# Fourteen warm-up products, delta rule output woven into the attention loop, and alternating 32x32 products in a hybrid decoder block

## The chip, the core and the metric

The kernel runs on one core of a Trainium2 chip. The metric is the device time of one execution in microseconds (us), as the median of several runs. A profile of one execution comes with it. In it PE is TensorE (matmuls), PEld its weight loads, DVE is VectorE, ACT is ScalarE, POOL is GpSimd, and SP is the engine from which nearly all transfers are issued.

## The reference

A decoder block on 512 tokens of width 1024, with 16 learned tokens ahead of them (528 in all): a gated feed-forward layer, a mixer, a second feed-forward layer and a norm. The mixer has two branches on the same normalised input.

```python
h = h + 0.5 * swiglu(rmsnorm(h, ffn1_norm), ...)            # FFN 1, hidden size 2816
u = rmsnorm(h, mix_norm)
c_q, c_kv, k_rope, g_q, g_k, g_v, g_b, g_a, g_z, gate_mla, gate_gdn = split(u @ w_in)
y_mla = mla(c_q, c_kv, k_rope, ...) @ w_mla_o               # 8 heads, causal softmax attention
y_gdn = gated_deltanet(g_q, ..., g_z, ...) @ w_gdn_o        # 8 heads of 64, chunked delta rule
h = h + (sigmoid(gate_mla) * y_mla + sigmoid(gate_gdn) * y_gdn) @ w_out
h = h + 0.5 * swiglu(rmsnorm(h, ffn2_norm), ...)            # FFN 2
# inside gated_deltanet, for each chunk: a triangular system tmat = (I + L)^-1, then
v_new = u_i - w_i @ state
o_i = (q_i * exp(g_i)) @ state + a_i @ v_new
state = state * exp(g_last) + k_dec^T @ v_new
# and at its end
o = rmsnorm(o, gdn_norm) * silu(z)
```

## The kernel before

All tensors lie with channels on the 128 partitions and tokens along the free dimension. A float32 product is made of three products of rounded parts: `weights` casts a slab of weights to its high part `whi` on ACT (L173) and makes the low part `wlo` on DVE (L174), and `mm3` (L201) issues high by high, high by low and low by high. The ring of slabs has three `whi` and three `wlo`, so a new slab's parts wait until the products with the slab three before are through.

The program runs through FFN 1 (to about 370 us), the mixer (to 735), the two branch projections with the gates and the output projection (to 825), FFN 2 (to 1173) and the last norm. Within the mixer the source gives every piece of work a place in a list of slots; a scheduler then writes the order of each engine by the priorities, and a table HOLD adds to it: ('kk', 0, 6, 30) says that the group named kk, number 0, stands behind the matmul with index 30 of input projection 6. Each engine runs its own list in order.

The parts that the change touches:

- The start. Eight products of a block of ones (`warm`, L517) stand ahead of FFN 1's first product `gu`, whose operands `ra` ACT makes from the loaded input (L279). In FFN 1's first tiles four `ssq` products (L268) stand between the `gu` products; they need `sqa`, the sum of the squares of the eight input tiles, made by ACT (`sq`, L235), POOL (L240) and DVE (L248 to L262).
- The output gate z of the delta rule: four projections `z`, each evicted from PSUM by DVE (L651), passed through Silu on ACT, multiplied by the norm's gain `gn` on POOL (L653), and stored to DRAM as `zd`. Their PSUM tile is one of a ring of two ("mm"), their SBUF tile one of a ring of three ("tA").
- `rope_key` rotates the shared key's 32 rows, in halves of 16 partitions: six DVE operations.
- `lower(c)` makes L of chunk c from eight small products `kk` (L872). `solve` inverts its 16x16 blocks by steps of two DVE operations (L895, L897). `merge` builds the inverses of two chunks each from those blocks, with 32x32 products `z1` (L932) and `x12` (L947, L951): all of row group 0 to 31 first, then all of row group 64 to 95. It is called for chunks 1 and 2, and for 3 and 4.
- `scan(c)` is one step of the recurrence: `ks`, then `rr`, eight DVE operations of 64 columns (L976), then `vn`, `oi`, `su`.
- `scan_out()` stands behind the last scan: for each of the four chunks the output `bv` is scaled (L1035), transposed by four products into `yT` (L1040), a PSUM tile of one buffer ("tk"), multiplied with z (`zs`, L1041), and stored as `yd`.
- `attention()` loops over 36 turns of five key blocks each for eight heads: `scores` (products `s`, L1154 to L1159, into the two-buffered PSUM tile "mm"; DVE evicts them to `pr`, L1160), `turn` (transposes `pt`, L1192, L1196), `values` (`o`). Between them it draws single steps of the gate projections (`gate`), whose PSUM tile ("ax") has one buffer and is evicted by DVE to `gt` (L1245).

Of the kernel before, what the change touches and what calls it, by code (L numbers as in the profile page):

```python
# [17 lines left out]
P = 128  # L18
# [22 lines left out]
ROPE = 12.5  # L41
NTAG = {"tA": 3, "tB": 3, "tC": 3, "tD": 4, "kb": 10, "rr": 1, "vn": 2, "vk": 1, "m": 4}
TAG = {n: t for t, ns in {
# [22 lines left out]
CYCLE = (0, 1, 2)  # L66
HOLD = (('nm', 0, 0, 32), ('nm', 1, 0, 36), ('b', 0, 1, 36), ('g', 0, 2, 42), ('tok', 1, 4, 5), ('tok', 2, 5, 4), ('tok', 3, 6, 2), ('tok', 4, 8, 21), ('tok', 7, 10, 0), ('sq', 0, 11, 25), ('vn', 0, 16, 14), ('kvn', 0, 14, 12), ('kvn', 1, 14, 18))
GX = (1,) * 16
# [16 lines left out]
def toff(c):  # L85
    return 0 if c == 0 else NM + P * (c - 1)
# [6 lines left out]
def build(tc, a, out, tap=None):  # L93
# [3 lines left out]
    with ctx:  # L97
# [408 lines left out]
        with tc.tile_pool(name="hid", bufs=1) as hid, tc.tile_pool(name="fp", bufs=2) as fp:  # L506
# [8 lines left out]
            warm = ax_tile("warm")  # L515
            for _ in range(8):
                nc.tensor.matmul(warm[:, 0:P], lhsT=ones, rhs=ones, start=True, stop=True)  # L517
# [130 lines left out]
        def z_tile(i):  # L648
            ps = proj(ZW + i, "z", SEQ)
            z = tmp("z")  # L650
            nc.vector.tensor_tensor(out=z, in0=ps, in1=r[:, NM:NT], op=ALU.mult)  # L651
            table(z, z, AF.Silu)
            nc.gpsimd.tensor_tensor(out=z, in0=z, in1=col("gn").broadcast_to([P, SEQ]), op=ALU.mult)  # L653
            dq.dma_start(zd[i], z)
# [95 lines left out]
        def rope_key():  # L750
            cosk, sink = tmp("cosk", NT, 48), tmp("sink", NT, 48)
            dq.dma_start(cosk, a["cosk"])
            dq.dma_start(sink, a["sink"])
            for x in range(2):
                e1, e2 = tmp("kr1", NT, NM), tmp("kr2", NT, NM)
                m1, m2 = (misc[0:16], misc[32:48])[::1 - 2 * x]
                o1, o2 = ((0, 16), (32, 48))[::1 - 2 * x]
                nc.vector.tensor_tensor(out=e1, in0=m1, in1=cosk[o1[0]:o1[1]], op=ALU.mult)
                nc.vector.tensor_tensor(out=e2, in0=m2, in1=sink[o2[0]:o2[1]], op=ALU.mult)
                nc.vector.tensor_tensor(out=e1, in0=e1, in1=e2, op=ALU.add if x else ALU.subtract)  # L760
                dq.dma_start(krd[16 * x:16 * x + 16], e1)

# [102 lines left out]
        def lower(c):  # L865
# [3 lines left out]
            for h4 in range(4):  # L869
                for hq, ps in enumerate(pk):  # L870
                    h = 2 * h4 + hq
                    nc.tensor.matmul(ps[0:n, h4, 0:n], lhsT=hs(kT, h, o, o + n), rhs=hs(kT, h, o, o + n), start=True, stop=True)  # L872
            for hq, ps in enumerate(pk):
# [36 lines left out]
        def merge(cs):  # L910
# [16 lines left out]
            z1 = sm_tile("z1").rearrange("p (k h s) -> p k h s", k=nk, h=H)  # L927
            for p in range(2):
                s1, s2 = slice(64 * p, 64 * p + 32), slice(64 * p + 32, 64 * p + 64)
                for k, c in enumerate(cs):  # L930
                    for h in range(H):
                        nc.tensor.matmul(z1[s1, k, h], lhsT=L[c][s2, h, s1], rhs=xt[s2, k, h], start=True, stop=True)  # L932
# [9 lines left out]
            x12 = sm_tile("x12").rearrange("p (k h s) -> p k h s", k=nk, h=H)  # L942
            for p in range(2):
                s1, s2 = slice(64 * p, 64 * p + 32), slice(64 * p + 32, 64 * p + 64)
                for k in range(nk):
                    for h in range(H):
                        nc.tensor.matmul(x12[s1, k, h], lhsT=tb[s1, k, h], rhs=nz[s1, k, h], start=True, stop=True)  # L947
                if p == 0:
                    for k in range(nk):
                        for h in range(H):  # L950
                            nc.tensor.matmul(x12[s2, k, h], lhsT=nz[s1, k, h], rhs=tb[s1, k, h], start=True, stop=True)  # L951
                    nc.vector.tensor_copy(t64[32:64, :, :, 0:32], x12[s2])
                for k, c in enumerate(cs):
                    ecopy(EM & 4)(X[c][s1, :, s2], x12[s1, k])
# [13 lines left out]
        def scan(c):  # L968
            n, o = tlen(c), toff(c)
            if c:  # L970
                psk = hd(tk_tile("ks"))
                rr = hd(tok("rr"))
                for i in range(4):
                    nc.tensor.matmul(psk[:, 2 * i:2 * i + 2], lhsT=kT[i][:, o:o + n], rhs=S[:, i], start=True, stop=True)
                for h in range(H):
                    nc.vector.scalar_tensor_tensor(out=rr[:, h], in0=psk[:, h], scalar=nbeg[:, c, h:h + 1],  # L976
                                                   in1=bv[c][:, h * 64:h * 64 + 64], op0=ALU.mult, op1=ALU.add)
                pso = hd(sm_tile("qs"))
# [51 lines left out]
        def scan_out():  # L1030
            nc.vector.scalar_tensor_tensor(out=ro, in0=ro, scalar=1.0 / 64, in1=sq_q[:, 1:5], op0=ALU.mult, op1=ALU.add)
            rsqrt(rn, ro, 1.0, False)
            for c in range(1, 5):
                o, o1 = toff(c), os_[c]
                nc.vector.tensor_tensor(out=o1, in0=o1, in1=hb(rn[:, c - 1], P), op=ALU.mult)  # L1035
                zs = tok("zs").rearrange("p (i t) -> p i t", i=4)
                dq.dma_start(zs, zd[:, :, o - NM:o - NM + P].rearrange("i p t -> p i t"))
                ps = tk_tile("yT").rearrange("p (i t) -> p i t", i=4)
                for i in range(4):
                    nc.tensor.transpose(out=ps[:, i], in_=o1[:, 2 * i:2 * i + 2].rearrange("p h d -> p (h d)"), identity=ident)  # L1040
                nc.vector.tensor_tensor(out=zs, in0=ps, in1=zs, op=ALU.mult)  # L1041
                dq.dma_start(yd[:, :, o - NM:o - NM + P].rearrange("i p t -> p i t"), zs)

# [34 lines left out]
        def keys_values():  # L1078
# [8 lines left out]
            for kc in range(5):  # L1087
# [5 lines left out]
                for i, (c, wk) in enumerate(((ck[0], kvh), (ck[1], kvh), (ck[0], kvl))):  # L1093
                    nc.tensor.matmul(ps, lhsT=c, rhs=wk[:, 4:8].rearrange("p a b -> p (a b)"), start=i == 0, stop=i == 2)
                v = tmp("v", SEQ, n)
# [156 lines left out]
        def attention():  # L1252
# [13 lines left out]
            for t in range(nst + LAG):  # L1266
# [10 lines left out]
                if i < 3:  # L1277
# [270 lines left out]
```

## Time and profile before

| | |
|---|---|
| median of 3 runs | 1191.19 us (1190.66 to 1191.98) |
| profiled execution: its own time | 1191.02 us |
| span of its trace | 1189.2 us |
| busy share of PE, PEld, DVE, ACT, POOL | 98%, 89%, 71%, 46%, 7% |

The span is the time between the first and the last record; the execution's own time has 1.8 us more around it. A record of the trace is one instruction; a float32 product of the small kinds (ones, 32x32) leaves two records. In the rows of a timeline the first number is the start, the second the length of the merged group including the last one's whole duration, and the brackets give the idle time of that engine just before it and who ended it.

### The profile page before, as it was taken

The page shows a single profiled execution, that of the slowest core. Times are in us where ns is not written, and L with a number is a line of the kernel's source. Part 1 is how long each engine was busy: PE and PEld are TensorE (multiplying, and loading weights), DVE is VectorE, ACT ScalarE, POOL GpSimd, SP SyncE. Part 2 cuts the span into 40 slices and gives each one's busy share as a digit, 9 for nine tenths or more (in the row PEclk, how much of TensorE's full clock was granted, in tenths as well). Part 3 has the DMA queues.
Part 4 walks back from the last instruction along what each step waited for, and adds up shares of the span by engine and source line. Part 5 has one row for each costly group of instructions (what it writes and reads, how often), then busy time and mean ns, then how long its engine had stood idle before and what let it go on. Part 6 is the DMA issues. An engine that isn't in the chain of part 4 may idle for free.

```text
span 1189.2 us, 20679 instructions
## 1 busy us (share of the span) xinstructions
PE 1169.6 (98%) x8108; PEld 1062.0 (89%) x8108; DVE 844.6 (71%) x1552; ACT 552.4 (46%) x974; POOL 89.2 (7%) x108
## 2 busy tenths in 40 slices
PE   9999999999999999999999999999999999999996
PEld 8999999999999999788877777878889999999985
DVE  5998787776655879973775555554979777886654
ACT  6544343433444574365334554434535433533444
POOL 1000000000002240101100001222000000000001
PEclk9999999999999999999999999999999999999999
DMA  6433332332234433354445434554533332233222
GB/s 238 126 114 101 107 107 90 106 95 84 94 112 162 150 76 104 109 169 138 147 141 148 134 125 133 177 186 146 199 124 107 107 96 99 90 107 107 80 80 71
DMA packets 69249, 145.37 MB, mean 122 GB/s; under 512 B 20032, under 2 KB 26512, under 8 KB 69152
## 3 DMA queue, kind: packets, MB, share of 16 engines
q1 hardware_dynamic: 68608, 143.52, 38.3%
q8 instruction: 64, 1.05, 0.4%
q10 hardware_dynamic: 544, 0.52, 0.1%
q14 instruction: 33, 0.27, 0.1%
HBM read 126.47 MB, written 17.55 MB: 121 GB/s over the span
## 4 chain that ended last, share of the span: by engine, by line
PE 50%; DVE 1%; ACT 0%; issue 0%; DVEq 0%
PE gu L436 14%; PE dn L201 10%; PE gate L201 6%; PE gu L201 6%; PE mo L201 4%; PE wo L201 4%; PE s L1157 1%; PE pt L1196 1%; PE o L1221 1%; PE s L1154 1%; PE qk L1015 1%; PE oi L1020 1%; PE qn L201 1%; PE o L1216 0%; PE vn L986 0%; DVE hk L1459 0%
## 5 line engine op out<-in xcount | busy, mean ns | idle before, releaser
L173 ACT CAST whi<-wraw 128x1024 fp32r<-128x1024 f32 (+1 forms) x125 | 127.2, 1017 | 193.3 <-issue 64.4
L174 DVE TENSOR_TENSOR wlo<-wraw,whi 128x1024 fp32r<-128x1024 f32 (+1 forms) x125 | 149.7, 1198 | 30.3 <-ACT whi L173 27.1
L436 PE MATMUL gu<-hd,form 128*128 128x264 f32 (+1 forms) x1152 | 154.6, 283 | 0.0
L436 PEld LDWEIGHTS gu<-hd,form 128*128 128x128 f32 x1152 | 146.6, 190 | 1.3
L288 ACT CAST form<-sf 128x512 fp32r<-128x512 f32 x128 | 78.6, 621 | 125.1 <-DVE sf L425 65.4
L341 DVE SCALAR_TENSOR_TENSOR hk<-dn,hk 128x528 f32<-128x528 f32 (+2 forms) x50 | 33.9, 677 | 108.1 <-PE dn L201 107.9
L436 PE MATMUL gu<-ut,form 128*128 128x264 f32 x768 | 101.1, 284 | 0.0
L436 PE MATMUL gu<-rb,form 128*128 128x256 f32 x768 | 100.0, 283 | 0.0
L201 PE MATMUL dn<-hd,whi 128*128 128x264 f32 (+2 forms) x372 | 98.4, 317 | 0.0
L288 ACT CAST form<-wraw 128x512 fp32r<-128x512 f32 x96 | 59.3, 620 | 83.1 <-PE gu L436 52.5
L436 PEld LDWEIGHTS gu<-ut,form 128*128 128x128 f32 x768 | 96.5, 188 | 0.0
L436 PEld LDWEIGHTS gu<-rb,form 128*128 128x128 f32 x768 | 95.6, 192 | 0.0
L289 DVE TENSOR_TENSOR form<-sf,form 128x512 fp32r<-128x512 f32 x128 | 87.0, 684 | 11.4 <-ACT form L288 11.3
L201 PE MATMUL gate<-ut,whi 128*128 128x512 f32 x256 | 88.2, 419 | 0.0
L201 PE MATMUL dn<-ra,whi 128*128 128x264 f32 x464 | 85.3, 285 | 0.0
L201 PE MATMUL dn<-ut,whi 128*128 128x512 f32 (+1 forms) x244 | 84.6, 384 | 0.0
L201 PE MATMUL dn<-ra,wlo 128*128 128x264 f32 x352 | 71.6, 285 | 0.0
L201 PE MATMUL dn<-ut,wlo 128*128 128x512 f32 (+1 forms) x188 | 71.4, 380 | 0.0
L289 DVE TENSOR_TENSOR form<-wraw,form 128x512 fp32r<-128x512 f32 x96 | 65.6, 685 | 6.4 <-ACT form L288 6.1
L201 PEld LDWEIGHTS dn<-ra,whi 128*128 128x128 f32 x464 | 68.5, 189 | 0.0
L201 PE MATMUL qkv<-ut,whi 128*128 128x264 f32 x384 | 66.1, 289 | 0.0
L201 PE MATMUL gu<-ra,whi 128*128 128x264 f32 x384 | 64.5, 291 | 1.7 <-ACT ra L279 1.7
(440 smaller groups left out, 2368.0 us busy)
## 6 DMA issues: line engine op xcount, KB each, us to landing
wraw<-w SPq DMA_DIRECT2D x86, 512.0 KB, 3.3
wraw<-win SPq DMA_DIRECT2D x36, 512.0 KB, 3.6
wraw<-d SPq DMA_DIRECT2D x32, 512.0 KB, 3.6
wraw<-d SPq DMA_DIRECT2D x16, 384.0 KB, 3.2
hk<-xT SPq DMA_DIRECT2D x16, 264.0 KB, 4.3
dec<-growd SPq DMA_DIRECT2D x8, 512.0 KB, 6.7
gated<-gt SPq DMA_DIRECT2D x16, 256.0 KB, 2.7
sg<-gated SPq DMA_DIRECT2D x16, 256.0 KB, 3.0
```

Of the source, the lines that this page charges most:

```text
L173: ih = nc.scalar.copy(hi[:, 0:n], raw[:, 0:n])
L174: il = (nc.gpsimd if pool_lo else nc.vector).tensor_tensor(out=lo[:, 0:n], in0=raw[:, 0:n], in1=hi[:, 0:n].bitcast(F32), op=ALU.subtract)
L201: trail.append(nc.tensor.matmul(o, lhsT=w, rhs=x[:, lo_:hi_], start=start and k == 0 and pi == 0, stop=stop and k == n - 1 and pi == 2).ins)
L288: nc.scalar.copy(hi, x)
L289: (eng or nc.vector).tensor_tensor(out=lo, in0=x, in1=hi.bitcast(F32), op=ALU.subtract)
L341: nc.vector.scalar_tensor_tensor(out=o, in0=p, scalar=0.5, in1=o, op0=ALU.mult, op1=ALU.add)
L436: nc.tensor.matmul(ps, lhsT=wt, rhs=xt, start=k == 0 and i == 0, stop=k == 3 and i == 2)
L1015: nc.tensor.matmul(ps[:, h4], lhsT=hs(kT, h, o, o + n), rhs=hs(qT, h, o, o + n), start=True, stop=True)
L1020: nc.tensor.matmul(psi[:, h], lhsT=e[:, h], rhs=vn[:, h], start=True, stop=True)
L1154: nc.tensor.matmul(ps[:, 0:w], lhsT=Q[h][:, b * P:(b + 1) * P], rhs=K[h][:, k0:k1], start=True, stop=True)
L1157: nc.tensor.matmul(ps[:, 0:t], lhsT=Q[h][:, b * P:(b + 1) * P], rhs=K[h][:, NM + k0:NM + k0 + t], start=True, stop=True)
L1196: nc.tensor.transpose(out=ps[:, b * P:(b + 1) * P], in_=Pr[h // 2, b][:, h % 2, NM * (h % 2) + c * P:NM * (h % 2) + (c + 1) * P], identity ...
```

## The change

- 14 products of ones ahead of FFN 1 in place of 8.
- The gain `gn` is multiplied in the last step of the delta rule (one DVE operation with both factors) instead of on POOL. `scan_out` keeps only the norm's factors; the rest is `scan_step(c)`, called in turns 0 to 3 of the attention loop. `yT` takes the two-buffered PSUM tile "sm".
- `rr` in two DVE operations of 512 columns; `rope_key` in four.
- `z1` and `x12` alternate between the row groups product by product; one copy (`t64`) stands behind all of `x12`.
- The ring "tA" has five buffers. HOLD: `tok` 1 stands further back in projection 4, `kk` 0 stands behind a product of projection 6, `x12` of chunk 1 behind a product of projection 20 (the first gate).

```diff
-NTAG = {"tA": 3, "tB": 3, "tC": 3, "tD": 4, "kb": 10, "rr": 1, "vn": 2, "vk": 1, "m": 4}
+NTAG = {"tA": 5, "tB": 3, "tC": 3, "tD": 4, "kb": 10, "rr": 1, "vn": 2, "vk": 1, "m": 4}
...
-HOLD = (('nm', 0, 0, 32), ('nm', 1, 0, 36), ('b', 0, 1, 36), ('g', 0, 2, 42), ('tok', 1, 4, 5), ('tok', 2, 5, 4), ('tok', 3, 6, 2), ('tok', 4, 8, 21), ('tok', 7, 10, 0), ('sq', 0, 11, 25), ('vn', 0, 16, 14), ('kvn', 0, 14, 12), ('kvn', 1, 14, 18))
+HOLD = (('nm', 0, 0, 32), ('nm', 1, 0, 36), ('b', 0, 1, 36), ('g', 0, 2, 42), ('tok', 1, 4, 16), ('tok', 2, 5, 4), ('tok', 3, 6, 2), ('tok', 4, 8, 21), ('tok', 7, 10, 0), ('kk', 0, 6, 30), ('x12', 1, 20, 7), ('sq', 0, 11, 25), ('vn', 0, 16, 14), ('kvn', 0, 14, 12), ('kvn', 1, 14, 18))
...
-            for _ in range(8):
+            for _ in range(14):
                 nc.tensor.matmul(warm[:, 0:P], lhsT=ones, rhs=ones, start=True, stop=True)
...
             table(z, z, AF.Silu)
-            nc.gpsimd.tensor_tensor(out=z, in0=z, in1=col("gn").broadcast_to([P, SEQ]), op=ALU.mult)
             dq.dma_start(zd[i], z)
...
+            e1, e2 = tmp("kr1", NT, 48), tmp("kr2", NT, 48)
+            nc.vector.tensor_tensor(out=e1, in0=misc[0:48], in1=cosk, op=ALU.mult)
+            nc.vector.tensor_tensor(out=e2, in0=misc[0:48], in1=sink, op=ALU.mult)
             for x in range(2):
-                e1, e2 = tmp("kr1", NT, NM), tmp("kr2", NT, NM)
-                m1, m2 = (misc[0:16], misc[32:48])[::1 - 2 * x]
-                o1, o2 = ((0, 16), (32, 48))[::1 - 2 * x]
-                nc.vector.tensor_tensor(out=e1, in0=m1, in1=cosk[o1[0]:o1[1]], op=ALU.mult)
-                nc.vector.tensor_tensor(out=e2, in0=m2, in1=sink[o2[0]:o2[1]], op=ALU.mult)
-                nc.vector.tensor_tensor(out=e1, in0=e1, in1=e2, op=ALU.add if x else ALU.subtract)
-                dq.dma_start(krd[16 * x:16 * x + 16], e1)
+                p, q = (slice(0, 16), slice(32, 48))[::1 - 2 * x]
+                nc.vector.tensor_tensor(out=e1[p], in0=e1[p], in1=e2[q], op=ALU.add if x else ALU.subtract)
+                dq.dma_start(krd[16 * x:16 * x + 16], e1[p])
...
-            for p in range(2):
-                s1, s2 = slice(64 * p, 64 * p + 32), slice(64 * p + 32, 64 * p + 64)
-                for k, c in enumerate(cs):
-                    for h in range(H):
+            rows = [(slice(64 * p, 64 * p + 32), slice(64 * p + 32, 64 * p + 64)) for p in range(2)]
+            for k, c in enumerate(cs):
+                for h in range(H):
+                    for s1, s2 in rows:
                         nc.tensor.matmul(z1[s1, k, h], lhsT=L[c][s2, h, s1], rhs=xt[s2, k, h], start=True, stop=True)
...
+            for k in range(nk):
+                for h in range(H):
+                    for s1, s2 in rows:
+                        mark("x12", cs[0], nc.tensor.matmul(x12[s1, k, h], lhsT=tb[s1, k, h], rhs=nz[s1, k, h], start=True, stop=True))
+                    (s1, s2), _ = rows
+                    mark("x12", cs[0], nc.tensor.matmul(x12[s2, k, h], lhsT=nz[s1, k, h], rhs=tb[s1, k, h], start=True, stop=True))
+            nc.vector.tensor_copy(t64[32:64, :, :, 0:32], x12[32:64])
...
-                for h in range(H):
-                    nc.vector.scalar_tensor_tensor(out=rr[:, h], in0=psk[:, h], scalar=nbeg[:, c, h:h + 1],
-                                                   in1=bv[c][:, h * 64:h * 64 + 64], op0=ALU.mult, op1=ALU.add)
+                nc.vector.tensor_tensor(out=rr, in0=psk, in1=hb(nbeg[:, c], P), op=ALU.mult)
+                nc.vector.tensor_tensor(out=rr, in0=rr, in1=hd(bv[c]), op=ALU.add)
...
-            for c in range(1, 5):
-                o, o1 = toff(c), os_[c]
-                nc.vector.tensor_tensor(out=o1, in0=o1, in1=hb(rn[:, c - 1], P), op=ALU.mult)
-                zs = tok("zs").rearrange("p (i t) -> p i t", i=4)
-                dq.dma_start(zs, zd[:, :, o - NM:o - NM + P].rearrange("i p t -> p i t"))
-                ps = tk_tile("yT").rearrange("p (i t) -> p i t", i=4)
-                for i in range(4):
-                    nc.tensor.transpose(out=ps[:, i], in_=o1[:, 2 * i:2 * i + 2].rearrange("p h d -> p (h d)"), identity=ident)
-                nc.vector.tensor_tensor(out=zs, in0=ps, in1=zs, op=ALU.mult)
-                dq.dma_start(yd[:, :, o - NM:o - NM + P].rearrange("i p t -> p i t"), zs)
+        def scan_step(c):
+            o, o1 = toff(c), os_[c]
+            nc.vector.tensor_tensor(out=o1, in0=o1, in1=hb(rn[:, c - 1], P), op=ALU.mult)
+            zs = tok("zs").rearrange("p (i t) -> p i t", i=4)
+            dq.dma_start(zs, zd[:, :, o - NM:o - NM + P].rearrange("i p t -> p i t"))
+            ps = sm_tile("yT").rearrange("p (i t) -> p i t", i=4)
+            for i in range(4):
+                nc.tensor.transpose(out=ps[:, i], in_=o1[:, 2 * i:2 * i + 2].rearrange("p h d -> p (h d)"), identity=ident)
+            nc.vector.scalar_tensor_tensor(out=zs, in0=ps, scalar=col("gn"), in1=zs, op0=ALU.mult, op1=ALU.mult)
+            dq.dma_start(yd[:, :, o - NM:o - NM + P].rearrange("i p t -> p i t"), zs)
...
+                if t < 4:
+                    scan_step(t + 1)
                 target = ngs * (t + 1) // (nst + LAG)
```

The order of PE around the first merge before: `z1` and `x12` are the 32x32 products, `v` are the attention's values, `gate` the gate projections; the last three rows stand in two places, 17 rows apart.

```order
L932 MATMUL z1_6675<-xt_6658,dec_5135 32x32 x8
L932 MATMUL z1_6675<-xt_6658,dec_5140 32x32 x8
L932 MATMUL z1_6675<-xt_6658,dec_5135 32x32 x8
L932 MATMUL z1_6675<-xt_6658,dec_5140 32x32 x8
...
L947 MATMUL x12_6720<-nz_6659,tb_6657 32x32 x16
L951 MATMUL x12_6720<-tb_6657,nz_6659 32x32 x16
...
L947 MATMUL x12_6720<-nz_6659,tb_6657 32x32 x16
```

And in the changed kernel, where the rows of x12 shown go on in the same way.

```order
L932 MATMUL z1_6673<-xt_6656,dec_5141 32x32 x16
L932 MATMUL z1_6673<-xt_6656,dec_5146 32x32 x16
...
L946 MATMUL x12_6718<-nz_6657,tb_6655 32x32 x2
L948 MATMUL x12_6718<-tb_6655,nz_6657 32x32
L946 MATMUL x12_6718<-nz_6657,tb_6655 32x32 x2
L948 MATMUL x12_6718<-tb_6655,nz_6657 32x32
```

The number of products is the same. In `z1` each row of 16 now holds both row groups in turn; in `x12` each two of L946 (one of each row group) are followed by one of L948.

The order of DVE between two evictions of z, before: L895 and L897 are the solve's steps, `rr` the scan's, `z` the eviction of the gate's projection. Where "..." is, steps of the solve and operations of rr alternate, 14 rows.

```order
L651 TENSOR_TENSOR z_5900<-z_5875,r_4624 128x512
L895 TENSOR_TENSOR rk_6532<-lt_6485,T_6486 128x255
L174 TENSOR_TENSOR wlo_6032<-wraw_6030,whi_6031 128x1024
L897 TENSOR_TENSOR T_6486<-T_6486,rk_6532 128x17x15
L976 SCALAR_TENSOR_TENSOR rr_6976<-ks_6975,nbeg_4689,bv_4679 128x64
...
L897 TENSOR_TENSOR T_6486<-T_6486,rk_6544 128x13x19
L651 TENSOR_TENSOR z_5936<-z_5911,r_4624 128x512
```

And in the changed kernel.

```order
L653 TENSOR_TENSOR z_5906<-z_5881,r_4630 128x512
L897 TENSOR_TENSOR T_6484<-T_6484,rk_6527 128x18x14
L973 TENSOR_TENSOR rr_6974<-ks_6973,nbeg_4695 128x512
L895 TENSOR_TENSOR rk_6530<-lt_6483,T_6484 128x255
L974 TENSOR_TENSOR rr_6974<-rr_6974,bv_4685 128x512
L897 TENSOR_TENSOR T_6484<-T_6484,rk_6530 128x17x15
L653 TENSOR_TENSOR z_5941<-z_5916,r_4630 128x512
```

Between the two evictions stood 19 operations; now five.

PE at the start of the attention loop before: `oi` are products of the last scan.

```order
L1015 MATMUL qk_7272<-qT3_4672,kT3_4668 128x128
L1020 MATMUL oi_7283<-vn_7256,dec_7258 128x64
L1157 MATMUL s_7361<-Kh_7346,Qh_7347 128x128
L1159 MATMUL s_7361<-Kh_7346,Qh_7347 128x16
L1157 MATMUL s_7366<-Kh_7346,Qh_7347 128x256
```

In the changed kernel: the end of one gate, two products of the next, and the first scores, which fill the two tiles of "mm" with the first two row pairs.

```order
L201 MATMUL gate_7396<-ut_4620,wlo_7392 128x512
L201 MATMUL gate_7533<-ut_4253,whi_7528 128x512
L201 MATMUL gate_7533<-ut_4254,whi_7528 128x512
L1154 MATMUL s_7295<-Kh_7280,Qh_7281 128x128
L1156 MATMUL s_7295<-Kh_7280,Qh_7281 128x16
L1154 MATMUL s_7300<-Kh_7280,Qh_7281 128x256
L1156 MATMUL s_7300<-Kh_7280,Qh_7281 128x16
L1154 MATMUL s_7306<-Kh_7280,Qh_7281 128x384
L1156 MATMUL s_7306<-Kh_7280,Qh_7281 128x16
L1154 MATMUL s_7312<-Kh_7280,Qh_7281 128x256
L201 MATMUL gate_7533<-ut_4253,wlo_7529 128x512
```

DVE at this place before: the last scan's operations and the first evictions of scores.

```order
L1017 TENSOR_TENSOR dec_7258<-qk_7272,dec_7258 128x4x128
L1160 ISA pr_7360,nb_4704<-s_7361,mS_4703 128x144
L1160 ISA nb_4704 128x1
L1160 ISA pr_7360,nb_4704<-s_7366,mS_4703 128x272
L1160 ISA nb_4704 128x1
L1021 TENSOR_TENSOR bv_4682<-oi_7283,bv_4682 128x512
```

And in the changed kernel: `gt_7506` empties the one-buffered PSUM tile that gate_7533 takes next, and `wlo_7692` takes the buffer of `wlo_7392`, the slab of gate_7396.

```order
L1032 TENSOR_TENSOR bv_4687<-bv_4687,rn_4706 128x512
L174 TENSOR_TENSOR wlo_7692<-wraw_7690,whi_7691 128x1024
L1242 TENSOR_TENSOR gt_7506<-gate_7396,r_4630 128x512
L1032 TENSOR_TENSOR bv_4688<-bv_4688,rn_4706 128x512
L1157 ISA pr_7294,nb_4710<-s_7295,mS_4709 128x144
L1157 ISA nb_4710 128x1
L1157 ISA pr_7294,nb_4710<-s_7300,mS_4709 128x272
```

Before, the first evictions of scores stood between the last scan's operations, and a wlo, the scaling of bv and the multiplications of zs came behind the scores of the first heads; now the whole of the last scan and three of the four scalings stand ahead, and that wlo, a gate's eviction and the fourth scaling stand directly ahead of the first `pr`. The four groups of yT, three of which stood within five rows of PE's list before, now stand 27, 22 and 12 rows apart.

## Rows read from the trace of the kernel before

**Rows 1.** The page: busy time by engine, share of the span, instructions.

```profile
PE 1169.6 (98%) x8108; PEld 1062.0 (89%) x8108; DVE 844.6 (71%) x1552; ACT 552.4 (46%) x974; POOL 89.2 (7%) x108
```

**Rows 2.** Waits of PE: for whom, us in total, times, longest us.

```profile
PE yT L1040 <- DVE zs L1041: 2.9, 2, 1.9
PE z L201 <- DVE z L651: 1.7, 1, 1.7
...
PE kk L872 <- ACT kT L147: 1.1, 1, 1.1
...
PE tok L785 <- ACT vT L147: 0.3, 1, 0.3
```

**Rows 3.** Timeline of PE, 0 to 28 us.

```profile
1.06 3.78 PE L517 MATMUL warm<-ones 128*128 128x128 f32 x16 [1.06 <-DVE epst L120]
6.51 1.61 PE L201 MATMUL gu<-ra,whi 128*128 128x264 f32 x5 [1.67 <-ACT ra L279]
...
11.66 0.64 PE L201 MATMUL gu<-ra,wlo 128*128 128x264 f32 x2
...
12.91 0.40 PE L201 MATMUL gu<-ra,wlo 128*128 128x264 f32 x2
...
27.09 1.13 PE L268 MATMUL ssq<-sqa,ones 128*128 128x264 f32 x4
```

**Rows 4.** Timelines of ACT and of DVE, 20 to 27 us.

```profile
20.41 1.05 ACT L173 CAST whi<-wraw 128x1024 fp32r<-128x1024 f32 x1 [1.14 <-PE gu L201]
...
26.23 0.71 DVE L262 TENSOR_TENSOR sqa<-sqa,sq 128x528 f32<-128x528 f32 x1
```

**Rows 5.** Timeline of PE, 523 to 534 us.

```profile
523.78 2.11 PE L932 MATMUL z<-xt,dec 32*32 32x32 f32 x64
...
528.08 0.21 PE L951 MATMUL x<-tb,nz 32*32 32x32 f32 x1
528.11 0.19 PE L947 MATMUL x<-nz,tb 32*32 32x32 f32 x1
528.13 0.19 PE L951 MATMUL x<-tb,nz 32*32 32x32 f32 x1
...
532.88 1.19 PE L947 MATMUL x<-nz,tb 32*32 32x32 f32 x32
```

**Rows 6.** Timeline of DVE, 484 to 492 us.

```profile
484.44 0.69 DVE L651 TENSOR_TENSOR z<-z,r 128x512 f32<-128x512 f32 x1
...
491.05 0.40 DVE L895 TENSOR_TENSOR rk<-lt,T 128x247 f32<-128x247 f32 x1
491.37 0.27 DVE L976 SCALAR_TENSOR_TENSOR rr<-ks,nbeg,bv 128x64 f32<-128x64 f32 x1
...
491.89 0.68 DVE L651 TENSOR_TENSOR z<-z,r 128x512 f32<-128x512 f32 x1
```

**Rows 7.** Timeline of PE, 613 to 625 us.

```profile
613.62 0.70 PE L201 MATMUL gate<-ut,whi 128*128 128x512 f32 x2
...
623.99 0.60 PE L1157 MATMUL s<-Kh,Qh 96*128 96x256 f32 x2
```

**Rows 8.** Stretches: length, then PE, PEld, DVE, ACT, POOL, clock, DMA.

```profile
621.00:623.00 2.00, 2.00 (x10) 1.81 (x9) 1.09 (x5) 0.73 (x2) 0.00 (x0) 0.50 1.12 363
```

**Rows 9.** Timeline of DVE, 605 to 621 us.

```profile
605.78 0.69 DVE L1017 TENSOR_TENSOR dec<-qk,dec 128x512 f32<-128x512 f32 x1 [2.76 <-PE qk L1015]
606.55 0.31 DVE L1160 CUSTOM_DVE_ANT_0 pr<-s,mS 128x144 f32<-128x144 f32 x1
...
616.31 1.22 DVE L174 TENSOR_TENSOR wlo<-wraw,whi 128x1024 fp32r<-128x1024 f32 x1
...
620.16 0.64 DVE L1245 TENSOR_TENSOR gt<-gate,r 128x512 f32<-128x512 f32 x1
```

**Rows 10.** The tile zs: its loads, and issue to landing.

```profile
L1037 SPq DMA_DIRECT2D zs<-zd x4: 424/486/1362, 565.6 to 568.0; - x4
...
DMA to landing us min/median/max: 2.2/4.9/7.5
```

More of the change, by code (lines that the diff above doesn't have):

```diff
@@ L629, in proj @@
                 ps = ax_tile(name)
+                trail.clear()
                 mm3([(ps, NM, NT)], w, us, True, True)
+                tiles[t] = list(trail)
                 return ps
@@ L871, in lower @@
                     h = 2 * h4 + hq
-                    nc.tensor.matmul(ps[0:n, h4, 0:n], lhsT=hs(kT, h, o, o + n), rhs=hs(kT, h, o, o + n), start=True, stop=True)
+                    mark("kk", c, nc.tensor.matmul(ps[0:n, h4, 0:n], lhsT=hs(kT, h, o, o + n), rhs=hs(kT, h, o, o + n), start=True, stop=True))
             for hq, ps in enumerate(pk):
@@ L942, in merge @@
             x12 = sm_tile("x12").rearrange("p (k h s) -> p k h s", k=nk, h=H)
-            for p in range(2):
-                s1, s2 = slice(64 * p, 64 * p + 32), slice(64 * p + 32, 64 * p + 64)
-                for k in range(nk):
-                    for h in range(H):
[L947 to L952, printed above, removed]
+            for k in range(nk):
[5 more added lines that the diff above has]
+            nc.vector.tensor_copy(t64[32:64, :, :, 0:32], x12[32:64])
+            for s1, s2 in rows[::-1]:
                 for k, c in enumerate(cs):
@@ L974, in scan @@
                     nc.tensor.matmul(psk[:, 2 * i:2 * i + 2], lhsT=kT[i][:, o:o + n], rhs=S[:, i], start=True, stop=True)
-                for h in range(H):
-                    nc.vector.scalar_tensor_tensor(out=rr[:, h], in0=psk[:, h], scalar=nbeg[:, c, h:h + 1],
-                                                   in1=bv[c][:, h * 64:h * 64 + 64], op0=ALU.mult, op1=ALU.add)
+                nc.vector.tensor_tensor(out=rr, in0=psk, in1=hb(nbeg[:, c], P), op=ALU.mult)
+                nc.vector.tensor_tensor(out=rr, in0=rr, in1=hd(bv[c]), op=ALU.add)
                 pso = hd(sm_tile("qs"))
@@ L1093, in keys_values @@
                 for i, (c, wk) in enumerate(((ck[0], kvh), (ck[1], kvh), (ck[0], kvl))):
-                    nc.tensor.matmul(ps, lhsT=c, rhs=wk[:, 4:8].rearrange("p a b -> p (a b)"), start=i == 0, stop=i == 2)
+                    mark("v", kc, nc.tensor.matmul(ps, lhsT=c, rhs=wk[:, 4:8].rearrange("p a b -> p (a b)"), start=i == 0, stop=i == 2))
                 v = tmp("v", SEQ, n)
```

## The prediction

> **What bounds the kernel now.** I read the page first: TensorE is busy for 98% of the span, VectorE for 71% [rows 1]. So an edit counts where it takes time from PE's own work, or from one of PE's few waits, and work taken off VectorE, ScalarE or GpSimd counts only as far as PE waits there. The list of PE's waits is short: 2.9 us for `zs`, 1.7 for `z`, 1.1 ahead of `kk`, 0.3 ahead of `tok` [rows 2], and 1.67 for `ra` at the start [rows 3]. The change touches each of these places. Then I read the timelines at them.
>
> **The start, eight to fourteen products of ones.** The products' 16 records run from 1.06 to 4.84 us; PE stands for 1.67 us, and begins `gu` at 6.51. A pair of `gu` records takes 0.64 us at 11.66 and 0.40 at 12.91, the same pair on either side of one step of the clock, from 1.2 to 2.4 GHz [rows 3]. Fourteen products leave 28 records, 28 x 0.22 = 6.2 us (3.78 for 16, with the last one's tail), which end at about 7.1 to 7.5: they cover the pause and delay `gu` by 0.6 to 1.0 us at most. If the clock rises because PE is busy without a break, it rises before 12.9, and each us earlier gives about half a us. All of that cannot be kept: `ssq` at 27.09 needs `sqa`, whose last addition ends at 26.94 (26.23 + 0.71) [rows 3, 4]. On the way to it only one wait is for PE: 1.14 us of ACT at 20.41 [rows 4]; the rest is POOL and ACT themselves. So the gain ends at 1.1 us. From there to 370 us PE has no listed wait, so what is won stays. I take 1.0; the bounds are +1.0 (the delay alone) and -1.2.
>
> **The holds (`tok`, `kk`).** Both products now stand where their operands are long made: 1.1 + 0.3 = 1.4 us of waits [rows 2]. I take 1.3 (0 to 1.4); what `kk` of the meta chunk feeds is first needed in a scan tens of us later.
>
> **z, rr, rope, the ring of five.** PE waits 1.7 us for the eviction of the second z at 491.89 [rows 2, 6]. The first was at 484.44, and 7.45 us of DVE's own list lie between: solve steps, `rr` and a `wlo`; a step and an `rr` start 0.32 and 0.20 us ahead of what follows. In the new order five operations lie between the two evictions, 3 x 0.40 + 2 x 0.69 = 2.6 us [rows 6, 9]. The wait goes; DVE may now wait for PE instead, and the solve behind it is no faster, but it has values and gates beside it on PE. I take 1.7. In each scan 8 x 0.20 = 1.6 us of `rr` become 2 x 0.69 = 1.4, two rope operations and POOL's four for z go too: small, and beside PE, so nothing beyond the wait. If the `z` wait stays, 0.
>
> **The 32x32 products.** The 64 records of `z1` take 2.11 us with the last one's 0.19, so 1.92 / 63 = 30 ns apart; the 32 of an `x12` group 1.00 / 31 = 32 ns [rows 5]. At the seam between two groups they interleave, 528.08, 528.11, 528.13: some 25 ns and less a record, with the `x12` of one line on either side of the other's [rows 5]. So a group alone seems bound by itself (weight load, then product, in the same part of the array), and two run side by side; I take half the pitch, 16 ns a record, as an estimate that the seam is too short to prove. In the new order `z1` takes 64 x 16 = 1.0 us instead of 1.9: 0.9. `x12` has 96 records, 96 x 32 = 3.1 us; at 16 ns 1.5, so 1.5 less. Two merges: 2 x (0.9 + 1.5) = 4.8 us, and PE is full there. The bounds are 0 (no overlap, or the inverses' own chain is late by as much) and 2 x (0.9 + 2.1) = 6.0, if all three groups of `x12` overlap. I take 4.5, as part of the second merge's `x12` is broken up by gates.
> The Trainium skill, TensorE: Matmul & The Clock Gate, Part 3 (The mechanism), says that a weight load overlaps running matmuls only where the row group differs; the trace disagrees in part, since the seam [rows 5] is between two groups of the same rows and different columns. By that rule each third product of `x12` would not be hidden, and the two merges would give about 3.8 us. Against the change speaks the Trainium skill, TensorEngine Tiling (Array Packing), Gotcha 1 (PSUM Pressure): different row tiles can't access the same PSUM bank at once, and `z1` and the first two products of `x12` do just that; that is the first rival below.
>
> **The delta rule's output in the attention loop.** Before, `yT` waited twice for `zs`, 1.9 and 1.0 us [rows 2], and after these the clock was at 0.50 from 621 to 623 [rows 8]; with the parts of the stretches beside it some 3.4 us, an estimate, half of which is lost: 1.7. Sum 2.9 + 1.7 = 4.6 us that go: the four groups now stand 12 to 27 rows apart, in a tile of two buffers.
> But something else comes to the head of the loop. The new orders show gate_7533 directly behind gate_7396, in the same one-buffered PSUM tile, and the eviction `gt_7506` behind `wlo_7692`, which itself needs the slab of gate_7396 to be through. From that gate's last product on: cast of `whi` 1.05 [rows 4], `wlo` 1.22, `gt` 0.64 [rows 9], with overlaps of 0.1 at each step about 2.8 us in which PE has nothing ahead. Then two gate products (0.70 with the tail of the last) and four scores (0.60 for two longer ones) [rows 7], while DVE does `bv`, 0.69 as any operation of that size, and `pr` 0.31 [rows 9]; the third score waits 0.1 to 0.4 more for its tile. So 3.0 us of new waiting. Before, the first scores were evicted between the last scan's operations [rows 9] and PE did not stand. The lower bound is 0.5 (the cast and `wlo` done sooner), the upper 4. A stop of 3 us may bring the clock down as at 620 (1.9 + 1.0 did): half a chance of 1.7, 0.8. So 4.6 - 3.0 - 0.8 = 0.8 gained. What is queued behind the waiting PE is all of the attention; behind `wlo_7692` on DVE the first `pr`.
>
> **New small waits.** Three of the scans now stand closer together, with less between `ks`, `rr` and `vn`, and four `zs` operations wait on DVE in the loop. I charge 1.0 us (0 to 4).
>
> **Sum.** 1.0 + 1.3 + 1.7 + 4.5 + 0.8 - 1.0 = 8.3 us. The profiled execution took 1191.02, its span 1189.2 and 1.8 around it; that is 0.17 below the median. 1191.02 - 8.3 = 1182.7, and on the median's footing 1182.9. I forecast 1183.
>
> **Rivals.**
> *The pairs don't overlap.* If products of two row groups into the same bank take turns, the 4.5 us stay out: 1187.5. Against it: a seam inside `z1` is within the same tile, and its 64 records took less (1.92) than 63 x 32 ns = 2.02 [rows 5]. The rule of Gotcha 1 in the Trainium skill's TensorEngine Tiling (Array Packing) would speak for it.
> *The scans' own chain comes out.* With the fillers gone from between, each of four scans shows part of its chain on PE. For it: in the trace DVE stands for PE up to 2.76 us there [rows 9], so both sides are tight. Two us a scan, eight in all, seven beyond what I charged, would give 1190; one us each, three beyond, 1186.
> *The clock at the start rises no earlier,* and fourteen products only delay `gu`: 1.0 gained becomes up to 1.0 lost, 1185.
> *Slower: the loads of z.* Before, the four `zs` loads were issued at 565.6 to 568.0, some 50 us ahead of their use, and took up to 7.5 us, 4.9 in the middle [rows 10]. Now each is issued in its turn of the loop, on SP behind the attention's other transfers, into a ring that `zs` shares with the attention's `phm` and `plm`. If each `zs` holds DVE, the scores' evictions behind it hold PE, once its two score tiles are full. With 4.9 us each, less 1.5 that PE has in hand, 4 x 3.4 = 13.6 us: 1183 + 13.6 = 1196.6. It decides from 8.3 / 4 = 2.1 us of PE per step on. Against it: at the first two steps the new order has much work between the load's turn and `zs`.
>
> **Chances.** The forecast's case, 1179 to 1185.5, 0.52 (with a clock that does not fall at the first scores, 1182); no overlap 0.14; scans or other new waits between 1185.5 and 1190 0.18; the start 0.08; slower by the loads 0.08. To leave out no more than 2 in 10 the range goes from 1178.5 to 1189.5. About 0.2% (2.4 us) is what a measurement of this kernel can tell from no change. Faster than 1188.8: 0.84; the same, 1188.8 to 1193.6: 0.09; slower: 0.07.
>
> **What would show it.** In the new profile: `gu` at 0.24 us for two records well before 12.9 and `ssq` near 26; no wait of PE for `kT`, `vT` or z's eviction; `z1` in about 1.2 us a merge and `x12` in about 1.7 where it runs in one piece; no wait for `zs` near 620, and one of about 3 us for `gt` or `pr` at the first scores, perhaps with a clock of 0.50 behind it. I would be wrong with `z1` still at 2 us, with PE waits at `vn` or `ks`, or with waits of DVE for `zs` loads and of PE for `pr` through the first turns.

## The result, and the profile after

The changed kernel takes 1199.65 us in the median of 20 runs (1190.54 to 1203.46), the kernel before 1190.66 in 20 (1189.57 to 1193.02): slower, with a ratio of 1.0067 (95% interval 1.0052 to 1.0082). The forecast was 1183, with a range that ended at 1189.5. The profiled execution took 1202.01 us, with a span of 1200.2 and a mean granted clock of 0.983; the one of before has 0.996. The spread is itself a result: 20 runs of before lie within 3.5 us, 20 of the changed kernel within 13.

The page of the changed kernel, against [rows 1], with its line of the granted clock in 40 equal slices:

```profile
PE 1177.7 (98%) x8120; PEld 1066.5 (89%) x8120; DVE 841.4 (70%) x1526; ACT 551.9 (46%) x974; POOL 83.7 (7%) x104
...
PEclk9999999999999999997989999999999999999999
```

The waits of PE, against [rows 2]:

```profile
PE gate L201 <- DVE gt L1242: 3.5, 2, 2.8
PE z L957 <- ACT X L952: 3.0, 2, 2.6
PE ssq L268 <- DVE sqa L262: 1.3, 1, 1.3
...
PE tok L785 <- ACT kT L147: 0.9, 1, 0.9
PE gate L201 <- DVE gt L647: 0.8, 1, 0.8
...
PE tok L785 <- ACT vT L147: 0.3, 1, 0.3
```

The waits for `zs`, `z` and `kk` are gone; in their place stand one for the first gate's eviction, 2.8 us, and one for the copies `X` of the second merge, 2.6 us. The line of the clock has two dips that the page of before has not. Stretches of the trace (length; busy time of PE, PEld, DVE, ACT, POOL; clock; DMA) show how long they are:

```profile
478.00:480.00 2.00, 2.00 (x7) 1.54 (x6) 1.84 (x2) 0.00 (x0) 0.00 (x0) 0.50 0.08 17
548.00:552.00 4.00, 2.14 (x38) 1.45 (x26) 1.21 (x2) 2.47 (x9) 2.52 (x2) 1.00 0.71 244
552.00:556.00 4.00, 3.24 (x20) 2.96 (x20) 0.68 (x1) 3.58 (x12) 0.00 (x0) 0.58 0.10 37
556.00:560.00 4.00, 4.00 (x35) 3.33 (x34) 0.10 (x1) 0.92 (x3) 1.09 (x1) 0.50 0.29 105
...
568.00:573.00 5.00, 5.00 (x20) 4.26 (x20) 1.29 (x2) 0.48 (x2) 0.00 (x0) 0.50 0.01 3
573.00:576.00 3.00, 3.00 (x26) 2.92 (x26) 2.07 (x3) 0.00 (x0) 0.00 (x0) 0.98 0.00 0
614.00:618.00 4.00, 1.24 (x6) 0.72 (x5) 3.83 (x6) 1.04 (x1) 0.00 (x0) 0.94 0.46 168
618.00:626.00 8.00, 8.00 (x22) 6.33 (x23) 2.10 (x9) 1.84 (x6) 0.00 (x0) 0.50 0.69 226
```

PE stands for half of 548 to 552, and then its clock is at 0.50 until about 573; it stands again at 615 to 617.7, and the clock is at 0.50 until about 627. With 478 to 481, before which PE did not stand, some 34 us run at half speed and cost 17. Before, it was one stretch of 3.4 us there [rows 8].

That the clock makes the spread can be read without any trace, from the span and the mean granted clock that come with every run: span times clock is, as an estimate, the time at full clock. Over the 20 runs the time goes from 1190.54 (clock 0.993) to 1203.46 (0.982), and span times clock only from 1178.5 to 1180.6, with a median of 1179.6. For 24 runs of the kernel before it is 1183.5 (1181.4 to 1185.2). By these medians the change gains 3.9 us at full clock; the clock takes 18 us where it took 6 before, and 3.9 - 12 comes near the measured loss of 9. But the estimate itself falls with the clock: the 24 runs of before give 1183.4 to 1185.2 at a clock of 0.996 and 1181.5 to 1182.1 at 0.992. The two runs of the changed kernel at 0.993 give 1180.4 and 1180.6, so at like clock the gain is nearer 1 to 2 us, and 3.9 is its upper end.

What made the two stops, from the timelines of ACT, PE and DVE:

```profile
549.51 2.45 ACT L147 ACTIVATE dec<-dec,ngc 128x128 f32<-128x128 f32 x8 [1.89 <-POOL dec L848]
551.98 1.27 ACT L952 COPY X<-x 32x256 f32<-32x256 f32 x4
...
614.62 0.39 PE L201 MATMUL gate<-ut,wlo 128*128 128x512 f32 x1
617.77 1.22 PE L201 MATMUL gate<-ut,whi 128*128 128x512 f32 x2 [2.76 <-DVE gt L1242]
...
615.89 1.22 DVE L174 TENSOR_TENSOR wlo<-wraw,whi 128x1024 fp32r<-128x1024 f32 x1 [0.17 <-ACT whi L173]
617.03 0.68 DVE L1242 TENSOR_TENSOR gt<-gate,r 128x512 f32<-128x512 f32 x1
```

The last `x12` product was through at 548.3, but the copies `X` that `z2` reads stood on ACT behind eight exponentials `dec` of a scan, which waited for POOL, and POOL for a load of `growd`. The second stop is the one that the orders had shown: cast, `wlo`, `gt`.

The other steps, against [rows 3, 5]:

```profile
1.06 5.97 PE L517 MATMUL warm<-ones 128*128 128x128 f32 x28 [1.06 <-DVE epst L120]
6.79 0.88 PE L201 MATMUL gu<-ra,whi 128*128 128x264 f32 x5
7.51 0.40 PE L201 MATMUL gu<-ra,wlo 128*128 128x264 f32 x2
...
26.41 1.13 PE L268 MATMUL ssq<-sqa,ones 128*128 128x264 f32 x4 [1.30 <-DVE sqa L262]
...
407.67 0.66 PE L785 MATMUL tok<-ident,kT 128*128 128x128 f32 x4 [0.91 <-ACT kT L147]
...
521.86 1.20 PE L932 MATMUL z<-xt,dec 32*32 32x32 f32 x64
...
525.84 0.22 PE L946 MATMUL x<-nz,tb 32*32 32x32 f32 x2
525.85 0.21 PE L948 MATMUL x<-tb,nz 32*32 32x32 f32 x1
...
526.85 0.19 PE L948 MATMUL x<-tb,nz 32*32 32x32 f32 x1
```

From the first `gu` on the pair of records takes 0.40 us. `z1` is down from 2.11 to 1.20 us, and all 96 records of `x12` stand between 525.84 and 526.85, 11 ns apart on average.

### The profile page after: what moved, and what is told of

Its sections match the earlier page's. It is cut to its first block, busy times and chain, and to the rows that moved or that the text cites. A ratio compares the mean times of both kernels' runs of the same rounds, so it can differ in the third digit from the quotient of the medians.

```text
span 1200.2 us, 20661 instructions
## 1 busy us (share of the span) xinstructions
PE 1177.7 (98%) x8120; PEld 1066.5 (89%) x8120; DVE 841.4 (70%) x1526; ACT 551.9 (46%) x974; POOL 83.7 (7%) x104
## 4 chain that ended last, share of the span: by engine, by line
PE 89%; DVE 3%; ACT 3%; DMA 3%; issue 1%; POOL 0%; SPq 0%; DVEq 0%; ACTq 0%; POOLq 0%
PE gu L436 27%; PE dn L201 21%; PE gu L201 10%; PE gate L201 6%; PE wo L201 4%; PE qkv L201 4%; PE mo L201 3%; PE z L201 2%; PE s L1154 1%; ACT dec L147 1%; PE cq L201 1%; DMA hk<-xT 1%; PE s L1151 1%; PE qk L1012 1%; DVE wlo L174 1%
## 5 line engine op out<-in xcount | busy, mean ns | idle before, releaser
L201 PEld LDWEIGHTS dn<-hd,whi 128*128 128x128 f32 x372 | 62.1, 189 | 4.2
```

What stands on the lines that cost most here:

```text
L201: trail.append(nc.tensor.matmul(o, lhsT=w, rhs=x[:, lo_:hi_], start=start and k == 0 and pi == 0, stop=stop and k == n - 1 and pi == 2).ins)
```

## The experiments

All ratios stand against runs of the kernel before on the same chip (that of e8 leaves out its longest run); "full" is the median of span times clock. The changed kernel itself was not run again beside them. The medians of before in the four sets are 1190.66 to 1191.93 us, so a difference between an experiment and the changed kernel carries up to 1.3 us of that.

| run | median, us (lowest to highest, runs) | ratio (95% interval) | clock, median | full, us |
|---|---|---|---|---|
| changed kernel | 1199.65 (1190.54 to 1203.46, 20) | 1.0067 (1.0052 to 1.0082) | 0.985 | 1179.6 |
| e1: ones ahead of z2 | 1191.18 (1188.94 to 1196.57, 11) | 1.0003 (0.9992 to 1.0014) | 0.994 | 1182.2 |
| e2: ones in both stops | 1188.27 (1186.61 to 1190.96, 7) | 0.9970 (0.9959 to 0.9981) | 0.996 | 1182.3 |
| e3: copies X on VectorE | 1184.80 (1182.27 to 1185.05, 5) | 0.9939 (0.9928 to 0.9951) | 0.996 | 1178.3 |
| e4: gate's eviction first | 1194.75 (1190.81 to 1202.25, 12) | 1.0035 (1.0019 to 1.0052) | 0.9875 | 1179.3 |
| e5: merges as before | 1186.62 (1185.16 to 1188.97, 5) | 0.9965 (0.9953 to 0.9976) | 0.996 | 1180.1 |
| e6: output as before | 1196.81 (1196.06 to 1199.95, 5) | 1.0053 (1.0041 to 1.0065) | 0.986 | 1178.2 |
| e7: before, alternating | 1186.39 (1184.81 to 1200.50, 12) | 0.9991 (0.9963 to 1.0018) | 0.995 | 1179.6 |
| e8: eight ones | 1196.47 (1184.78 to 1207.68, 12) | 1.0036 (1.0010 to 1.0063) | 0.9885 | 1180.4 |
| e9: ones behind the stop | 1198.18 (1196.89 to 1199.18, 4) | 1.0060 (1.0045 to 1.0075) | 0.991 | 1185.4 |
| e10: e3, tok held | 1183.42 (1181.80 to 1195.10, 12) | 0.9955 (0.9930 to 0.9980) | 0.997 | 1178.1 |

**Is it the stop, the clock, or the small products?** The stops were filled with products that nothing reads, and the rest of each engine's order stayed as it was (in e2 all but a few rows in the attention).

```diff
# e1; HOLD gets ('fill', 0, 22, 6), behind the gate product that stands ahead of the stop
                 ps = hd(sm_tile("z2"))
+                if c == 3:
+                    for _ in range(12):
+                        mark("fill", 0, nc.tensor.matmul(ps[:, 0:2], lhsT=ones, rhs=ones, start=True, stop=True))
# e2: also, in gate_steps, behind the first gate's last product and ahead of the second's first
+                if j == ng[0] + 1:
+                    wps = tk_tile("warm2")
+                    for _ in range(13):
+                        wi = nc.tensor.matmul(wps[:, 0:P], lhsT=ones, rhs=ones, start=True, stop=True).ins
```

> Twelve products of ones (2.6 us at full clock) stand in PE's order directly ahead of the first z2 of the second merge, where PE waits 2.6 us for the copies X; nothing else of any engine's order moves. They change no wait that sets an end. Theory A (the stop lets TensorE's clock fall, and the half clock from 552 to 573 us is what costs): the clock stays at 1.00 there, about 10 us are won, near 1189.5 us. Theory B (the clock falls because merge and scans hold little but small products, with or without the stop): it falls all the same within some us after 552, time within 3 us of the changed kernel's 1199.6. Theory C (the waits themselves cost, not the clock): no change, 1199.6.

> As the run before, and thirteen products of ones more between the two gates at the head of the attention loop, where PE waits 2.8 us for the eviction of the first gate. Theory A: both half-clock stretches (20 and 10 us) are gone, 15 us won, near 1184.5 us, both waits being still there but filled. Theory B: the second stretch (dense gate products) may stay full, the first falls: near 1195. Theory C: no change.

e1 brought 8.5 us with twelve products of no use, as theory A has it. It refutes C, since `z2` begins no sooner: 3.50 us behind the start of the last gate product ahead of the stop, against 3.02 in the changed kernel. The stop in e1's timeline of PE:

```profile
549.53 2.83 PE L958 MATMUL z<-ones 128*128 128x128 f32 x23 [0.23 <-issue]
552.30 1.14 PE L960 MATMUL z<-X,dec 64*64 64x64 f32 x16
```

And its stretches, where the changed kernel had a clock of 0.58 and 0.50:

```profile
552.00:556.00 4.00, 4.00 (x53) 3.37 (x52) 0.68 (x1) 2.30 (x8) 0.00 (x0) 1.00 0.37 111
556.00:560.00 4.00, 4.00 (x38) 3.23 (x37) 1.65 (x5) 1.80 (x6) 1.24 (x2) 1.00 0.40 152
```

The same merge and scans run at full clock, so B is not the cause of this fall. The products were not free: in that execution the copies X began 1.54 us behind the same gate product (2.24 in the changed kernel), and `z2` had to wait until the ones were through.

e2 won 2.9 more, less than the 5 forecast. In its median run the clock is not the reason (0.996); its time at full clock is 1182.3, as e1's is 1182.2, 2.6 above the changed kernel's estimate, by the ones that run on and by waits that the changed kernel's profile doesn't have (`gu` for `whi` L187, 1.0 and 1.2 us). How much each of these costs is not shown. In e2's profile, the slowest of its seven runs, the clock fell elsewhere, from 534 to 545, where the longest wait ahead of it was 0.6 us. So B has its part: the clock can fall with hardly a stop. Theory A holds for the two large dips, not for each one.

**Taking the stops away.**

```diff
# e3
-EM = 0
+EM = 4      # copies X from x12 on VectorE
# e4, in gate_steps: the low part that takes gate j's slab stands behind gate j's eviction
+                if len(gts) > 2:
+                    behind(last_split[1], gts[-3])
...
-                nc.vector.tensor_tensor(out=t, in0=ps, in1=r[:, NM:NT], op=ALU.mult)
+                gts.append(nc.vector.tensor_tensor(out=t, in0=ps, in1=r[:, NM:NT], op=ALU.mult).ins)
```

> The copies X of both merges go to VectorE instead of ScalarE, where they stand behind eight exponentials; no wait for them is left. The scheduler also puts the first gate's eviction ahead of the next wlo here, so the stop at the first scores shrinks from 2.8 to about 0.8 us. Theory A: 2.6 + 2 us of waits and 15 us of half clock go: 1180 to 1184. Theory B: the waits go, the clock falls in the scans all the same: about 1193. Theory C: 1199.6 - 4.6 = 1195.

> Each gate's eviction stands ahead of the wlo that takes over the slab of the same gate; the merge is as in the changed kernel. The stop at the first scores shrinks to about 0.8 us; the stop ahead of z2 stays. Theory A: 2 us of wait and 5 us of half clock go, the stretch from 552 to 573 stays: about 1193. Theory B: the same or less, 1193 to 1198. Theory C: 1197.6.

e3's waits of PE:

```profile
PE ssq L268 <- DVE sqa L262: 1.9, 1, 1.9
PE tok L785 <- ACT kT L147: 1.5, 2, 1.0
PE z L957 <- DVE X L952: 1.2, 2, 0.7
...
PE gate L201 <- DVE gt L1242: 0.9, 1, 0.9
```

Both stops are below 1 us and the time is 1184.8, 0.8 us above the forecast's upper end. Of the 14.9 us to the changed kernel some 13 are clock: 4.7 us are lost to it in the median run, against 18. e4 keeps the stop ahead of `z2`, and with it a dip from 552 to 580 in its profile; it wins 4.9. Its stop at the first scores is still 1.4 us, not 0.8, and 2.5 us of new waits for `zs` came up; its time lies in the ranges of A and B and doesn't tell them apart.

**Which part of the change brought the stops?**

```diff
# e6
             rsqrt(rn, ro, 1.0, False)
+            for c in range(1, 5):
+                scan_step(c)
...
-            ps = sm_tile("yT").rearrange("p (i t) -> p i t", i=4)
+            ps = tk_tile("yT").rearrange("p (i t) -> p i t", i=4)
...
-                if t < 4:
-                    scan_step(t + 1)
# e8
-            for _ in range(14):
+            for _ in range(8):
```

e5 is the changed kernel with the lines of `z1`, `x12`, `t64` and the copies X of the kernel before, and without the hold on `x12`; e7 is the kernel before with those lines of the changed one and nothing else. Their lines are those of the diff ahead of the prediction.

> The changed kernel with the merges as before: groups one after the other, copy t64 after the first two groups, no hold on x12. The new order of ScalarE has copies X ahead of the second batch of exponentials again, and the first scores stand between the last scan's operations as before. Theory A2 (the shorter merges made the scheduler move other work, and that made both stops): neither stop is there, 5.9 us of products come back and 5.4 us of waits go, and the clock loses what it lost before the change: about 1186. Theory D (the stop at the first scores is from the output steps in the loop): the 2.8 us stop and its half clock stay, about 1193.

> The changed kernel with the delta rule's output all behind the last scan as before, in its one-buffered tile. Theory A2: the stop ahead of z2 is the same, and the four yT at the head of the loop wait for zs again as before: 1199 to 1202. Theory D: the stop at the first scores is gone with its half clock: about 1193.

> The kernel before with the alternating products of both merges alone (and the copy t64 behind all of x12). Its new order has the copies X behind eight exponentials, as the changed kernel. Theory A2: 5.9 us of products are saved, a stop of 2 to 3 us ahead of z2 comes with 10 us lost at half clock: 1195 to 1199. Rival E (alternating is a plain gain, and another part made the stop): 1185.

> The changed kernel with eight products of ones. Nothing else of any order moves. The step of the start: ssq at 27.1 instead of 26.4 us, the clock rising near 12.9 instead of before 7; 0.7 us more at full clock, which the spread of the times covers: 1200. If fourteen products do nothing, ssq stands at 26.4 too.

e5 came out as A2 had it, 1186.6: with the old merges neither of the two stops is there; the longest wait at a gate is 1.5 us.

```profile
PE gate L201 <- DVE gt L1244: 1.5, 1, 1.5
```

e6, with the output as before, has the stop ahead of `z2`, and `yT` waits for `zs` again:

```profile
PE z L957 <- ACT X L952: 3.1, 2, 2.7
PE yT L1039 <- DVE zs L1040: 2.4, 1, 2.4
```

So the stop ahead of `z2` comes with the alternating order, through the schedule. Theory D is half right: the stop at the first scores needs both parts. In e6 no gate waits for the first gate's eviction any more. The wait for `zs` in its place brought no fall in that profile, and 1196.8 lies between what D and A2 expected. At full clock e6 has 1178.2, so the output's new place gains nothing there.

e7 divides between A2 and E. Seven runs lie at 1184.8 to 1186.6, five at 1192.1 to 1200.5, and span times clock is 1179.6 (1176.9 to 1180.8), 4 us under before's. Its waits:

```profile
PE z L201 <- DVE z L651: 1.7, 1, 1.7
PE z L957 <- ACT X L952: 1.7, 1, 1.7
```

The stop ahead of `z2` is there, but shorter, and the clock fell by more than usual (0.991 or lower) in 5 of 12 runs. In the changed kernel, with 2.6, it was below 0.992 in 18 of 20; in e3, with 0.7, in none of 5. In e4, with 2.6 too, it was so in 10 of 12. The expectation of e7, a sure fall, was wrong: the longer the stop ahead of `z2`, by one profile for each kernel, the more often the clock fell. The length is not all: e10 below, with 0.5, has 3 of 12.

e8 shows the ones alone, from its timeline (the rest of that execution, the longest of its runs, is not used):

```profile
1.06 3.79 PE L517 MATMUL warm<-ones 128*128 128x128 f32 x16 [1.06 <-DVE epst L120]
...
12.02 0.64 PE L201 MATMUL gu<-ra,wlo 128*128 128x264 f32 x2
...
13.17 0.40 PE L201 MATMUL gu<-ra,wlo 128*128 128x264 f32 x2
...
27.36 0.91 PE L268 MATMUL ssq<-sqa,ones 128*128 128x264 f32 x3
```

`ssq` is back at 27.4. The time at full clock is 0.8 us more than with fourteen, but over a spread of 5.6 us; neither that nor the medians can tell.

**Why does the clock stay low for 20 us?**

```diff
# e9; HOLD gets ('fill', 0, 22, 10)
                 ps = hd(sm_tile("z2"))
+                if c == 4:
+                    for _ in range(24):
+                        mark("fill", 0, nc.tensor.matmul(ps[:, 0:2], lhsT=ones, rhs=ones, start=True, stop=True))
```

> Twenty-four products of ones (5.1 us at full clock, 10.2 at half) stand behind the stop this time, after the first z3 of the second merge, near 557 us, with the stop ahead of z2 as in the changed kernel. It asks why the clock stayed low for 20 us there. Theory G1 (the small products of merge and scans keep it low): the dense products bring it back before the scans begin, within 10 us of its fall; about 8 us are added and 5 or more won back, near 1202. Theory G2 (how long it stays low has nothing to do with what PE runs): it comes back some 20 us after the fall or later, and the time is near 1209.

The timeline of PE in e9:

```profile
551.52 1.45 PE L960 MATMUL z<-X,dec 64*64 64x64 f32 x16 [2.44 <-ACT X L952]
556.81 8.22 PE L958 MATMUL z<-ones 128*128 128x128 f32 x48
```

Its stretches behind that:

```profile
560.00:564.00 4.00, 4.00 (x28) 4.00 (x28) 0.00 (x0) 0.24 (x1) 0.00 (x0) 0.71 0.00 0
564.00:568.00 4.00, 4.00 (x44) 3.36 (x43) 0.68 (x1) 0.00 (x0) 0.00 (x0) 1.00 0.21 66
...
614.00:618.00 4.00, 1.23 (x7) 0.67 (x5) 3.79 (x7) 1.05 (x1) 0.00 (x0) 1.00 0.53 186
618.00:626.00 8.00, 8.00 (x40) 6.63 (x41) 3.08 (x13) 2.77 (x9) 0.00 (x0) 1.00 0.69 219
```

The same stop, the same fall; but the clock is back before 563, within the dense products, and stays at 1.00 through merge and scans. The kernel does 5 us more and is no slower than the changed one (1.0060 against 1.0067). G1 holds here: what followed the stop in the changed kernel, mostly products of 64 rows or 64 columns, kept the clock low. The time is 3.8 us under G1's forecast. In this profile the second stop, 2.8 us as in the changed kernel, brought no fall at all (the last two rows), so a stop of that length is no sure fall either. Why the clock took 10 us to come back behind that stop in the changed kernel, where gate products stood, is open.

**A version that beats both.** e10 is e3 with `('tok', 2, 5, 14), ('tok', 3, 6, 8)` in HOLD.

> The kernel with copies X on VectorE (1184.8), and the groups tok 2 and tok 3 held 10 and 6 products further back, where PE waited 1.0 and 0.5 us for kT. If these waits are plain waits, 1.2 us are won: 1183.5; if the wait only moves to what stands next (as the hold of kk moved it from kk to tok), nothing.

1183.4 in the median, as expected, but the wait only half went: in its profile PE waits 1.2 us at `kk` for `cx`. Three of its 12 runs lie at 1194.6 to 1195.1 with a clock of 0.986 to 0.988, so the clock's risk is not gone, and its lead over e3 is not settled. e3 is 0.61% under the kernel before, e10 0.45% by the ratio over its runs.

## Why the prediction was wrong

The step that failed is the price of the clock: 0.8 us in the sum, where 12 us more than before were lost in the median run, most of it behind two stops, one of them not in the sum at all.

**The start** held: the clock rose before 7.5 us and `ssq` came 0.68 us earlier (27.09 to 26.41), held by `sqa` as said; I took 1.0.

**The holds** were mis-sized: `kk` no longer waits for `kT`, but that `kT` is also what `tok` reads next, 0.91 us at 407.67, and `tok` waits 0.3 for `vT` as before. Of 1.3 us at most 0.2 came. A wait for data that others need is not won by moving one reader.

**z** held: 1.7 us are gone.

**The 32x32 products** gave more than I took: `z1` 0.9 and `x12` about 2.1 a merge, 6 us for both, the upper bound, since all three groups of `x12` run side by side. The rival of no overlap is refuted. But I worked out that step for PE alone. I had the order of PE around the merges and did not follow what reads `x12`: the copies X, all of which now stand behind the whole of `x12`, moved behind eight exponentials on ACT. Which part of the new order moved them was not tested by itself. The line "the inverses' own chain is late by as much" was a bound, and no price was put on it.

**The output in the loop** failed, and with it the forecast. The wait at the first scores is 2.8 us where I had 2.8 to 3.0. The price of the clock behind it was "half a chance of 1.7, 0.8"; it is 9.7 us at half clock in the profile, about 5 lost. I sized it by the one fall that the trace of before shows, 3.4 us long, and charged it to one stop. With the stop that I missed the clock cost 12 us more than before. e1 to e4 showed that: fill the stops or shorten them, and 5 to 15 us come back.

**New waits**: a charge of 1.0 against 3.0 for X and 0.8 for another gate. Neither `ks`, `rr` nor the loads of z stood in the way: the loads took 2.3 to 2.6 us, and PE waited for none of the three.

Summed at full clock, with the waits as listed: 0.7 + 0.2 + 1.7 + 6.0 + 2.9 for `yT`, less 3.5 + 3.0 + 0.8, is 4.2; span times clock gives 3.9, and less at like clock. The list of gains was right in the main. What was missing is that a stop of 2 to 3 us has to be priced with the clock that may follow it.

## What to carry to other kernels

On an engine that is busy for 98%, look for stops of 2 to 3 us in the new order ahead of stretches of small products, and price each with the half clock that may follow, not with its own length. When products get shorter, follow their readers on the other engines, in the new order there: what used to be covered by the slow products is the next wait. Where a stop can't be removed, products that nothing reads can hold the clock, as in e1 and e2, and cost what they run beyond the stop. Multiply span by granted clock for each run before explaining a spread, and compare kernels only at like clock.

## What the hardware showed that was not expected

Products of 32x32 in two row groups, written to one shared bank, ran side by side in `z1` at 16 ns a record; with a third group of the same rows and other columns between them, in `x12`, at 11 ns; against 30 to 32 for one group [rows 5]. The Trainium skill, TensorEngine Tiling (Array Packing), Gotcha 1 (PSUM Pressure), says that different row tiles can't access the same PSUM bank at once; no such turns show here. But the two row groups also differ in their columns (in `z1` they are rows 32 to 63 and 96 to 127, written to partitions 0 to 31 and 64 to 95), and two over the same columns were not run. The Trainium skill, TensorE: Matmul & The Clock Gate, Part 3 (The mechanism), says that a weight load overlaps running products only where the row group differs. By that a third of the products of `x12` would have stayed in line, some 2 us a merge as an estimate, and it took 1.0.

The clock also fell without a stop: near 478 us in the profiles of the changed kernel, e3, e4, e6 and e9, behind products of 16 rows or 2 columns with PE busy throughout, and in e2 at 534, behind a wait of 0.6 us. In those of before, e1, e2, e5, e7 and e10 it did not fall at 478, with much the same products there. What decides it in a given execution stays open.
